# Convolution block 1 as four plain stretches ahead of the heads, with all of x prepared beside them

## The chip, the cores and the metric

One core of one Trainium2 chip runs the whole kernel. The metric is the device time of one execution in microseconds; the profile is one profiled execution on that core. Its engines are TensorE (PE), VectorE (DVE), ScalarE (ACT), GpSimd (POOL) and SyncE (SP), whose queue issues nearly all transfers of this kernel.

## The reference

One layer over 2048 tokens of width 1024, with 256 context tokens and a conditioning vector:

```python
shift, scale, gate = split(silu(c) @ w_ada + b_ada, 3)
h  = rmsnorm(x, norm_w) * (1 + scale) + shift
hc = rmsnorm(ctx, norm_w) * (1 + scale_c) + shift_c
p, pc = h @ w_in, hc @ w_in[:, :5 * 1024]        # w_in: 1024 x 9216
# 8 heads of 128: q, v, f_f, f_b and a gate; a gated linear recurrence in both directions,
# its start state from the context
y_hg = norm(o) * silu(gate)
# 8 convolution blocks of 128 channels, columns h, b, c, gate:
y_cv = b * conv3(c * h, along rows of 64) * silu(gate)
x = x + gate * (concat(y_hg, y_cv) @ w_out)
return rmsnorm(x, final_norm_w)
```

## The kernel before

The tokens stand in four groups of 512 (x0 to x3). Each group's normed h is transposed, so that a product has 128 columns of w_in as weights and tokens as the moving side. Every number is kept as two f16 parts (hi and lo), and a product is three f16 matmuls: hi·hi, hi·lo, lo·hi.

Two columns of 128 against the two halves of a group form a 2x2 block product, done in one of two ways. *Seven* (function `seven`) is a Strassen form: seven products instead of eight, on sums of weights (A11, A12, A22, S1 to S4) and sums of tokens: B11, T1, T2, B21, T3, B22, T4. A unit of seven is 7 x 4 x 3 = 84 matmuls, 256 wide in a head stretch; in a "pair" stretch of the convolution two groups run together, 512 wide. *Plain* needs no sums, only the hi and lo of h itself.

The token operands of the sevens lie in DRAM (`Hd`, rows of them by `ROWS`). A stretch loads its seven in "hops" of 512 KB ahead of use (`prefetch`; nine places). They are made from h32 by DVE subtractions and by casts on ACT or POOL: `turn` for a group that comes fresh from its transposes, `late_turn` for one whose h32 was put into DRAM (`Xd`) and is loaded again. Each has eight k-steps for D of 1024, or four pairs k, k+4: four (late) turns per group.

The program is a list of stretches ("windows"), and each has PE units, the chain of the scan and extra steps (norms, turns, weights' preparation), which are dealt out among the matmuls at fixed shares of the stretch. What is written in that order stands in that order on each engine, and every engine runs its row in order. Stretches 0 to 3 are head 0 on groups 0 to 3, then heads 1 to 7, convolution block 0 (four stretches), and blocks 1 to 7 as two "pair" stretches each. Head 0's stretches 0 and 1 are plain (256 wide) out of tiles in SBUF, since the sevens' operands do not exist yet; beside them x1 to x3 and the context are normed and turned, and scans of head 0 run. Groups 0 and 1 get their T operands by late turns in stretches 3 to 6. `gate_sums` (the residual's gate, eight `wg` loads of 512 KB, four with PE sums `gate_r` in stretch 2's first part and four in its second) run beside. Results leave PSUM by ACT (p, u) and by DVE (f, z, K and others); PE can use a bank again after that.

Names: `xT_x` transposes; `h_x` normed groups; `hop2T`: hop of stretch 2, T row; `sa`, `sb`, `sc`: banks of sevens; `u`: bank of plain or context products; `ws_p`: weights from DRAM; `whia_p`, `wloa_p`, `e_p` and so on: their parts; `ss_p`: the small matmul for a pair's scale; `ha_x`, `hb_x`, `hc_x`: what late turns load; `hpT_x`: what they store.

Of the kernel before, what the change touches and what calls it, by code (L numbers as in the profile page):

```python
# [31 lines left out]
VQ_AT = 3  # L32
SMALL = {"cc": 16, "bada": 16, "nw": 8, "lg": 32, "onw": 1, "cw": 24}
# [27 lines left out]
def hybrid_layer(ctx: ExitStack, tc, x, cx, w_ada, b_ada, w_in, w_out, fnorm_w, small_d, masks, ident_d, sel_d, out):  # L61
# [19 lines left out]
    ROWS = (("B11", "T3"), ("T1", "T2"), ("B21", "B22"), ("T4",))  # L81
# [3 lines left out]
    Xd = [dp.tile([P, KT, GW], F32, name=f"Xd{g}", tag=f"Xd{g}") for g in range(2)]  # L85
# [155 lines left out]
    def norm_group(ntile, src, row0, m, nm, first_ops=None, space=q_tile):  # L241
# [4 lines left out]
        before = None if opening else "x0" if m else f"x{row0 // GW - 1}"  # L246
# [58 lines left out]
        def store(op, k, src, eng):  # L305
            if m:
                i = ("B1", "B2", "D").index(op)
                hi, lo = hc[:, i, 0, k], hc[:, i, 1, k]
            else:
                hi, lo = [first_ops[k // 2][:, k % 2, i] for i in range(2)]  # L310
            cast(eng, hi, src)
            low.append(V.tensor_tensor(lo, src, hi, ALU.subtract))

        def store2(ops, k, row, eng):

            n2 = len(ops)
            pair = hp.tile([P, n2, 2, HW], F16, tag="pair", name=f"hp{ops[0]}_{nm}{k}", bufs=4)
            hi, lo = pair[:, :, 0], pair[:, :, 1]
            row = row.rearrange("p (a b) -> p a b", a=n2)
            cast(eng, hi, row)  # L320
            low.append(V.tensor_tensor(lo, row, hi, ALU.subtract))
            g = row0 // GW
            if n2 == 2:
                SY.dma_start(Hr[g][ops][:, :, k], pair)
            else:
                SY.dma_start(Hd[g][ops[0]][:, k], pair[:, 0])

        made = {}

        def rows_ahead(k):  # L330
            made[k] = rows(k), rows(k + HK)

        def turn(k):
            a, b = made.pop(k) if k in made else (rows(k), rows(k + HK))
# [7 lines left out]
            if first_ops is not None:  # L342
                for kk, h32 in ((k, a), (k + HK, b)):
                    SY.dma_start(Xd[row0 // GW][:, kk], h32)
                    store(None, kk, h32, S if kk < HK else G)
                return
            combine(k, a, b, True)

        def late_turn(k):
            a, b = ring(f"ha_{nm}{k}"), ring(f"hb_{nm}{k}")  # L350
            for kk, h32 in ((k, a), (k + HK, b)):
                SY.dma_start(h32, Xd[row0 // GW][:, kk])
            combine(k, a, b, False)
            late_done[row0 // GW] += 1
            prefetch()

        def combine(k, a, b, whole):
            b11, b12, b21, b22 = a[:, :HW], a[:, HW:], b[:, :HW], b[:, HW:]
            t = ring(f"ht_{nm}{k}")
            t1, t2 = t[:, :HW], t[:, HW:]  # L360
            V.tensor_tensor(t1, b12, b11, ALU.subtract)
# [8 lines left out]
            V.tensor_tensor(b21, b21, t2, ALU.subtract)  # L370
            store2(("T4",), k, b21, G)
# [5 lines left out]
                [lambda k=k: raw(k, pa_t if k < KT - 2 else px_t) for k in range(KT)],  # L377
                [paced(0.0, lambda k=k: rows_ahead(k)) for k in range(HK)])
# [16 lines left out]
    def load_pair(col0, col1, nm, own=False, a21_at=None):  # L395
# [47 lines left out]
        def sum_b():  # L443
# [4 lines left out]
                  part("S2", lambda: a11), sum_b, part("S3", lambda: a21), part("S4", lambda: a12)]  # L448
        block = col0 // P - 5 * HEADS
# [389 lines left out]
    class Conv:  # L839


        def __init__(s, b, groups):
            s.b, s.groups, s.nm = b, groups, f"{b}_{groups[0]}"
            s.n = HW * len(groups)
            s.cv = [None, None]
# [4 lines left out]
        def conv(s, i, u):  # L850
# [8 lines left out]
                                   ALU.mult, ALU.add)  # L859

# [366 lines left out]
    for wi, (kind, a, i) in enumerate(stretch):  # L1227
        units, chain, extra = [], [], []
        if kind == "head":
# [28 lines left out]
        else:
# [41 lines left out]
        if kind == "pair":  # L1300
            n = (a - 1) * 2 + i
# [91 lines left out]
    late_done = {0: 0, 1: 0}  # L1393
    plain = [[hp.tile([P, 2, 2, GW], F16, tag="hop", name=f"hop{g}_{i}") for i in range(KT // 2)] for g in range(2)]
    x1_norm = norm_group(NCH, x, GW, 0, "x1", plain[1], stage_tile)
    a21_ = hop_tile("a21")
    ga21 = scp.tile([P, 2, HK, P], F16, tag="Tsec", name="ga21", bufs=5)
    extra_a21 = [[[a21_[:, :, hl, i * P:(i + 1) * P] for hl in range(2)] for i in range(2)], [[ga21[:, 0], ga21[:, 1]]]]
    taken[0] = HOPS

    first = norm_group(NCH, x, 0, 0, "x0", plain[0])
# [10 lines left out]
    ctx_norm = norm_group(2, cx, 0, 1, "c")  # L1412
    for _, st in ctx_norm[0] + x1_norm[0]:
# [34 lines left out]
    def cost(u):  # L1448
        return {"head": 7 * HK, "conv": 7 * HK, "ctx": KT, "plain": 2 * KT, "pair": 14 * HK}[u[1]]

    ui = 0

    def run(wi, units, steps):
        nonlocal ui
        total = sum(cost(u) for u in units) - (0 if units[-1][1] in ("ctx", "plain") else cost(units[-1]) // 7)
# [18 lines left out]
        for un, (wk, kind, i, fn) in enumerate(units):  # L1474
# [22 lines left out]
            elif kind == "plain":  # L1497
                ps = bank(turn_bank[0], f"u{ui}")
# [186 lines left out]
```

## Time and profile before

| | us |
|---|---|
| median of three runs | 2150.36 (2148.98 to 2151.59) |
| span of the profiled execution | 2150.1 |
| PE busy | 2073.2 (96%) |
| DVE busy | 1645.8 (77%) |
| ACT busy | 1192.2 (55%) |
| POOL busy | 191.8 (9%) |
| mean granted TensorE clock | 0.994 |

Rows of groups and of the timeline give the time (or the count and busy time), the engine, the line of the kernel, the operation, what it writes and reads, and in brackets how long the engine was idle ahead of it and what ended that. A matmul's own duration overlaps that of the next; the distance of two starts is its price. Line numbers are those of the kernel before; the changed kernel's are a few to sixteen higher.

### The profile page before, as it was taken

The numbers are of one execution on the slowest core, as the hardware profiler recorded it, in microseconds if no ns is written. First come the engines' busy times: TensorE is split into PE (matmuls) and PEld (weight loads), VectorE is DVE, ScalarE is ACT, GpSimd is POOL, SyncE is SP. The second block draws the span as 40 slices with busy tenths as digits, with TensorE's granted clock in tenths as the row PEclk, the third lists the DMA queues.
The fourth block names the chain that finished last, engine by engine and source line by source line (L and its number), as shares of the span: only waits on it lengthen the run. The fifth ranks groups of instructions, "written<-read, shape, count | busy, mean of one in ns | idle before, by whom it ended". The sixth has DMA issues, their size and how long they took to land.

```text
span 2150.1 us, 53050 instructions
## 1 busy us (share of the span) xinstructions
PE 2073.2 (96%) x22111; PEld 1466.0 (68%) x22111; DVE 1645.8 (77%) x3413; ACT 1192.2 (55%) x2406; POOL 191.8 (9%) x272
## 2 busy tenths in 40 slices
PE   5988999999999999999999999999999999999998
PEld 2877878888888888888888887444444444444443
DVE  6787988878778787788687887678778656687775
ACT  7965666757567666576676654354445423333332
POOL 0121111111111110111110100000000000000000
PEclk9999999999999999999999999999999999999999
DMA  9567533442344233424543458933442105642421
GB/s 356 191 207 265 178 126 134 137 158 72 114 129 146 97 114 109 153 81 142 194 131 127 130 165 260 285 108 110 134 149 93 54 23 196 206 143 92 137 79 59
DMA packets 185798, 311.02 MB, mean 145 GB/s; under 512 B 13010, under 2 KB 114770, under 8 KB 183764
## 3 DMA queue, kind: packets, MB, share of 16 engines
q1 hardware_dynamic: 183396, 303.68, 42.9%
q8 instruction: 173, 2.83, 0.5%
q10 hardware_dynamic: 2160, 3.93, 0.5%
q14 instruction: 69, 0.57, 0.1%
HBM read 240.19 MB, written 67.37 MB: 143 GB/s over the span
## 4 chain that ended last, share of the span: by engine, by line
PE 65%; DVE 18%; ACT 7%; DMA 4%; issue 3%; POOL 1%; SPq 0%; POOLq 0%; ACTq 0%; DVEq 0%
PE sa L930 8%; PE sa L932 8%; PE sa L931 8%; PE sb L930 4%; PE sb L932 4%; PE sb L931 4%; PE sa_o L930 2%; PE sa_o L931 2%; PE sa_o L932 2%; DVE Q L492 2%; PE sc L930 2%; PE sc L931 2%; PE sc L932 2%; DVE K L485 2%; PE T L681 2%
## 5 line engine op out<-in xcount | busy, mean ns | idle before, releaser
L931 PEld LDWEIGHTS <-e_p 128*128 128x128 f16 x1332 | 130.4, 98 | 59.8 <-issue 10.3
L930 PEld LDWEIGHTS <-e_p 128*128 128x128 f16 x1332 | 130.4, 98 | 54.0 <-issue 1.1
L601 ACT ACTIVATE km<-K 128x512 f32<-128x512 f32 x192 | 129.6, 675 | 67.2 <-DVE K L485 61.1
L932 PEld LDWEIGHTS <-e_p 128*128 128x128 f16 x1332 | 130.3, 98 | 51.4
L485 DVE TENSOR_TENSOR K<-K,tot 128x512 f32<-128x512 f32 x192 | 132.2, 689 | 42.9 <-ACT km L601 25.3
L492 DVE TENSOR_TENSOR Q<-Q,tot 128x512 f32<-128x512 f32 x192 | 132.5, 690 | 34.9 <-POOL qm L608 19.5
L608 POOL COPY qm<-Q 128x512 f32<-128x512 f32 x96 | 80.8, 842 | 794.4 <-DVE Q L492 778.7
L931 PEld LDWEIGHTS <-whib_p 128*128 128x128 f16 x888 | 86.9, 98 | 42.1 <-issue 8.8
L930 PEld LDWEIGHTS <-whib_p 128*128 128x128 f16 x888 | 86.8, 98 | 36.7 <-issue 0.8
L930 PEld LDWEIGHTS <-whia_p 128*128 128x128 f16 x888 | 87.0, 98 | 35.7 <-DMA hop3B<-Hd3B 2.3
L932 PEld LDWEIGHTS <-wloa_p 128*128 128x128 f16 x888 | 87.0, 98 | 34.2
L931 PEld LDWEIGHTS <-whia_p 128*128 128x128 f16 x888 | 87.0, 98 | 33.9 <-issue 1.5
L932 PEld LDWEIGHTS <-wlob_p 128*128 128x128 f16 x888 | 86.8, 98 | 34.0
L157 ACT ACTIVATE e_p<-ws_p,sc_p 128x512 f16<-128x512 f32 x108 | 77.5, 718 | 54.9 <-DVE ws_p L444 42.0
L665 POOL COPY A<-Ac 32x128 f32<-32x128 f32 x128 | 77.2, 603 | 128.3 <-ACT A L661 110.6
L853 ACT ACTIVATE cv<-c,small 128x512 f32<-128x512 f32 (+1 forms) x36 | 24.2, 673 | 106.8 <-DVE c L871 61.1
L937 ACT ACTIVATE u<-sa,sx_w 128x256 f32<-128x256 f32 (+1 forms) x111 | 58.1, 524 | 43.5 <-PE sa L932 34.7
L937 ACT ACTIVATE p<-sa,sx_w 128x256 f32<-128x256 f32 (+1 forms) x111 | 57.4, 517 | 39.9 <-PE sa L932 39.8
L158 DVE SCALAR_TENSOR_TENSOR e_p<-ws_p,sc_p,e_p 128x512 f16<-128x512 f32 x108 | 79.4, 750 | 0.0
L409 ACT ACTIVATE junk<-ws_p 128x1024 f16<-128x1024 f32 x72 | 75.7, 1052 | 6.5 <-DMA ws_p<-in_w_in 6.3
L1596 POOL TENSOR_TENSOR x_o<-x_o,fw 128x512 f32<-128x512 f32 x1 | 1.3, 1262 | 868.0 <-ACT junk L1587 868.0
L937 ACT ACTIVATE p<-sb,sx_w 128x256 f32<-128x256 f32 (+1 forms) x111 | 57.8, 521 | 30.8 <-PE sb L932 28.0
(858 smaller groups left out, 7036.3 us busy)
## 6 DMA issues: line engine op xcount, KB each, us to landing
ws_p<-in_w_in SPq DMA_DIRECT2D x72, 512.0 KB, 4.3
y_o<-yT SPq DMA_DIRECT2D x32, 512.0 KB, 4.3
xt_x<-in_x SPq DMA_DIRECT2D x16, 512.0 KB, 6.2
wa<-in_w_ada SPq DMA_DIRECT2D x16, 512.0 KB, 10.2
Gd<-zs SPq DMA_DIRECT2D x32, 256.0 KB, 2.7
sg<-Gd SPq DMA_DIRECT2D x32, 256.0 KB, 4.4
wos<-in_w_out SPq DMA_DIRECT2D x32, 256.0 KB, 5.0
yT<-y SPq DMA_DIRECT2D x32, 256.0 KB, 2.9
```

What stands on the lines that cost most here:

```text
L157: S.activation(hi, src, AF.Copy, scale=st[:, 0:1])
L158: V.scalar_tensor_tensor(lo, src, st[:, 0:1], hi, ALU.mult, ALU.subtract)
L409: S.activation(junk.rearrange("p (k n) -> p k n", k=KT), stage[i], AF.Abs, accum_out=r)
L485: V.tensor_tensor(m, m, sub(cur, nb + 1, [[2, np_], [-(nb + 1), 2], [0, B]]), ALU.mult)
L492: V.tensor_tensor(m, m, sub(cur, 1, [[2, np_], [nb - 1, 2], [0, B]]), ALU.mult)
L601: S.activation(sub(s.km, 0, [[2 * B, n // (2 * B)], [B, 2], [1, B]]), mix(s.K, n, B, n // (2 * B)), AF.Copy)
L608: G.tensor_copy(sub(qm, 0, [[2 * B, n // (2 * B)], [B, 2], [1, B]]), mix(s.qf, n, B, n // (2 * B)))
L665: G.tensor_copy(A3[js, :, js], s.Ac[js])
L930: PE.matmul(ps, hi[:, k], rh, start=start and k == 0, stop=False, skip_group_check=not start)
L931: PE.matmul(ps, hi[:, k], right(name, 1, k), start=False, stop=False, skip_group_check=not start)
L932: PE.matmul(ps, lo[:, k], rh, start=False, stop=k == nk - 1, skip_group_check=not start)
L937: last_keep.append(S.activation(r, ps, AF.Copy, scale=sx))
```

## The change

Block 1 of the convolution leaves the "pair" stretches and becomes four new stretches ("open") ahead of head 0, one for each group. Each has two units of two products, plain, 512 wide (8 x 3 = 24 matmuls a product), evacuated by `open_first` and `open_second`. Their weights are the plain hi and lo, in tiles borrowed from the scan's pools (`homes`). Beside the four stretches run x1, x2, x3 and the context's norms and turns: now every group is cast plainly, kept in `Xd` and stored as B11, B21, B22 (`store_plain`). All T operands of all four groups come from 16 late turns of a new form: four loads, DVE subtractions, one POOL subtraction, and all casts on POOL. They stand in stretches 1 to 6. Heads 0 to 7 follow as stretches 4 to 35, all with sevens; head 0's first stretch starts without scan work. `gate_sums` moves to the last part of stretch 3, and its last sums come in stretch 4's first unit.

```diff
-    ROWS = (("B11", "T3"), ("T1", "T2"), ("B21", "B22"), ("T4",))
+    ROWS = (("T4", "T2"), ("T1", "T3"), ("B11",), ("B21", "B22"))
...
         def late_turn(k):
+            g = row0 // GW
             a, b = ring(f"ha_{nm}{k}"), ring(f"hb_{nm}{k}")
-            for kk, h32 in ((k, a), (k + HK, b)):
-                SY.dma_start(h32, Xd[row0 // GW][:, kk])
-            combine(k, a, b, False)
+            c_ = u_tile(f"hc_{nm}{k}")
+            SY.dma_start(b, Xd[g][:, k])
+            for r in range(2):
+                SY.dma_start(a[:, r * HW:(r + 1) * HW], Xd[g][:, k + r * HK, HW:])
+            SY.dma_start(c_, Xd[g][:, k + HK, :HW])
+            V.tensor_tensor(b, a, b, ALU.subtract)
+            V.tensor_tensor(a[:, HW:], a[:, HW:], b[:, :HW], ALU.subtract)
+            store2(("T1", "T3"), k, b)
+            G.tensor_tensor(a[:, :HW], c_, a[:, HW:], ALU.subtract)
+            store2(("T4", "T2"), k, a)
...
-    stretch = [("head", hd, i) for hd in range(HEADS) for i in range(NG)]
+    stretch = [("open", OPEN_B, g) for g in range(NG)]
+    stretch += [("head", hd, i) for hd in range(HEADS) for i in range(NG)]
...
-    stretch += [("pair", b, tp) for b in range(1, 8) for tp in range(2)]
+    stretch += [("pair", b, tp) for b in range(OPEN_B + 1, 8) for tp in range(2)]
...
+        elif kind == "open":
+            units.append((wkey(c0 + 2 * 1024, c0), kind, i, cvx.open_first))
+            units.append((wkey(c0 + 1024, c0 + 3 * 1024), kind, i, cvx.open_second))
...
-            elif n == 10:
+            elif n == 9:
                 extra += gate_steps()
-            elif n == 13:
+            elif n == 11:
                 extra += [paced(w_, put_next) for w_ in (0.35, 0.35, 0.15, 0.15)]
...
-            elif kind == "plain":
...
+            elif kind == "open":
+                for r, put in enumerate(fn(w)):
+                    ps = bank(open_bank[0], f"u{ui}{r}")
...
+                        PE.matmul(ps, op[0][:, kk], rh[0], start=k == 0, stop=False)
+                        PE.matmul(ps, op[0][:, kk], rh[1], start=False, stop=False)
+                        PE.matmul(ps, op[1][:, kk], rh[0], start=False, stop=k == KT - 1)
...
             if wi == 0:
+                early += x1_norm[1] + x1_norm[2][:1] + x2_norm[0] + x1_norm[2][1:] + x2_norm[1][:-1]
             elif wi == 1:
+                early += x2_norm[1][-1:] + x3_norm[0] + x2_norm[2] + x3_norm[1][:-1] + late_[0][:2]
+            elif wi == 2:
+                stage_free.append(True)
+                next_w(0, 2)
+                early += x3_norm[1][-1:] + ctx_norm[0] + x3_norm[2] + ctx_norm[1][:-1] + late_[0][2:]
             else:
+                next_w(0, 2)
                 sums = gate_sums()
+                early += (ctx_norm[1][-1:] + ctx_norm[2] + sums[:1] + late_[1][:2] + sums[1:2] + late_[1][2:3]
+                          + sums[2:])
...
+        elif wi == NG:
+            extra = late_[1][3:] + late_[2][:2] + [paced(0.1, lambda: next_w(1, 1))] + late_[2][2:3] + extra
+        elif wi == NG + 1:
+            extra = late_[2][3:] + late_[3][:2] + extra
+        elif wi == NG + 2:
+            extra = late_[3][2:] + extra
```

In the rows that follow, a tile's name has its own number behind it. The four late turns of group 1 are called x10 to x13 (turns 0 to 3 in the prediction). DVE before, at the start of stretch 3: two evacuations of f (head 0, group 3), and between them late turn x10 among scan work.

```order
L941 SCALAR_TENSOR_TENSOR f_0_3_2573<-sa_16_2575,sx_w0_482,p5_16_2652 128x256
L361 TENSOR_TENSOR ht_x10_2622<-ha_x10_2618 128x256
L492 TENSOR_TENSOR Q_0_2_2411<-Q_0_2_2411,tot_0_2_2639 128x64x2x4
L362 TENSOR_TENSOR ht_x10_2622<-hb_x10_2619,ht_x10_2622 128x256
L364 TENSOR_TENSOR ha_x10_2618<-hb_x10_2619,ha_x10_2618 128x256
L370 TENSOR_TENSOR hb_x10_2619<-hb_x10_2619,ht_x10_2622 128x256
L639 COPY_PREDICATED Ac_0_2_2695<-mask_127,A2_0_2_2755 128x128
L321 TENSOR_TENSOR hpT1_x10_2625<-ht_x10_2622,hpT1_x10_2625 128x2x256
L321 TENSOR_TENSOR hpT3_x10_2630<-ha_x10_2618,hpT3_x10_2630 128x256
L321 TENSOR_TENSOR hpT4_x10_2635<-hb_x10_2619,hpT4_x10_2635 128x256
L639 COPY_PREDICATED Ac_0_2_2695<-mask_127,A2_0_2_2755 128x128
L941 SCALAR_TENSOR_TENSOR f_0_3_2573<-sb_16_2607,sx_w0_482,u2_16_2709 128x256
```

DVE after, from the second late turn of group 1 (x11) at the end of the opening to head 0's first evacuations of f; `sg_1_3` is the gate of the last opening product.

```order
L348 TENSOR_TENSOR hb_x11_1528<-ha_x11_1527,hb_x11_1528 128x512
L349 TENSOR_TENSOR ha_x11_1527<-ha_x11_1527,hb_x11_1528 128x256
L324 TENSOR_TENSOR hpT1_x11_1536<-hb_x11_1528,hpT1_x11_1536 128x2x256
L324 TENSOR_TENSOR hpT4_x11_1541<-ha_x11_1527,hpT4_x11_1541 128x2x256
L869 SCALAR_TENSOR_TENSOR sg_1_3_1608<-u71_1519,sx_w1_583,sg_1_3_1608 128x512
L348 TENSOR_TENSOR hb_x12_1572<-ha_x12_1571,hb_x12_1572 128x512
L870 TENSOR_TENSOR sg_1_3_1608<-sg_1_3_1608,cv0_1_3_1438 128x512
L349 TENSOR_TENSOR ha_x12_1571<-ha_x12_1571,hb_x12_1572 128x256
L324 TENSOR_TENSOR hpT1_x12_1580<-hb_x12_1572,hpT1_x12_1580 128x2x256
L871 TENSOR_REDUCE ymax_130<-sg_1_3_1608 128x2
L324 TENSOR_TENSOR hpT4_x12_1585<-ha_x12_1571,hpT4_x12_1585 128x2x256
L957 SCALAR_TENSOR_TENSOR f_0_0_1621<-sc_8_1689,sx_w8_1618,p1_8_1658 128x256
```

Two late turns (x11 and x12) now stand ahead of head 0's first evacuation f, with the opening's last gate between them, and a third (x13, the rows behind these) ahead of the second evacuation.

SP before, at the same place of stretch 3: two hop loads, the scan's Gd stores, and the loads of two late turns.

```order
L1389 DMA hop3B22_2564<-Hd3B21_101 128x2048
L1389 DMA hop3T4_2566<-Hd3T4_102 128x2048
L795 DMA Gd0_105<-zs0_2_2569 128x512
L795 DMA Gd1_106<-zs1_2_2601 128x512
L352 DMA ha_x10_2618<-Xd1_104 128x512
L352 DMA hb_x10_2619<-Xd1_104 128x512
L1389 DMA hop5B11_3323<-Hd2B11_95 128x2048
L352 DMA ha_x11_2823<-Xd1_104 128x512
L352 DMA hb_x11_2824<-Xd1_104 128x512
L1389 DMA hop5T1_3325<-Hd2T1_96 128x2048
```

SP after: the stores of late turn x11 (`Hd1T1`, `Hd1T4`), the last gate loads `wg6` and `wg7`, the loads and stores of x12, and the hops of head 0's first stretch (`hop4`) among them.

```order
L325 DMA Hd1T1_92<-hpT1_x11_1536 256x1x512
L325 DMA Hd1T4_91<-hpT4_x11_1541 256x1x512
L1096 DMA wg6_1566<-in_w_ada 128x1024
L1096 DMA wg7_1568<-in_w_ada 128x1024
L344 DMA hb_x12_1572<-Xd1_104 128x512
L346 DMA ha_x12_1571<-Xd1_104 128x256 x2
L347 DMA hc_x12_1573<-Xd1_104 128x256
L1399 DMA hop4B22_1614<-Hd0B21_90 128x2048
L1109 DMA Gr_139<-gate_rows_1603 128x512
L1399 DMA hop4T4_1616<-Hd0T4_87 128x2048
L325 DMA Hd1T1_92<-hpT1_x12_1580 256x1x512
L873 DMA yT3_118<-sg_1_3_1608 128x512
```

The loads of a late turn now stand behind the stores of the one before, with gate loads between them.

PE before, in stretch 2: gate sums behind transposes of x3, among products of T2.

```order
L274 MATMUL xT_x36_2221<-ident_121,xt_x30_1371 128x128
L274 MATMUL xT_x36_2221<-ident_121,xt_x31_1373 128x128
L274 MATMUL xT_x36_2221<-ident_121,xt_x32_1586 128x128
L274 MATMUL xT_x36_2221<-ident_121,xt_x33_1588 128x128
L1087 MATMUL gate_r_2228<-wg0_1871,sc32_124 32x512 x2
L1087 MATMUL gate_r_2228<-wg1_1873,sc32_124 32x512 x2
L1087 MATMUL gate_r_2228<-wg2_1875,sc32_124 32x512 x2
L1087 MATMUL gate_r_2228<-wg3_1877,sc32_124 32x512 x2
L930 LDWEIGHTS e_p8_274
```

PE after, in head 0's first stretch: the last four pairs of gate sums stand between the second product (`sc`, B21) and the third (`sa`, B11).

```order
L946 MATMUL sc_8_1689<-hop4B21_1277,whia_p24_1088 128x256
L947 LDWEIGHTS whia_p24_1088
L947 MATMUL sc_8_1689<-hop4B21_1277,whia_p24_1088 128x256
L948 LDWEIGHTS wloa_p24_1089
L948 MATMUL sc_8_1689<-hop4B21_1277,wloa_p24_1089 128x256
L1103 MATMUL gate_r_1553<-wg4_1562,sc32_126 32x512 x2
L1103 MATMUL gate_r_1553<-wg5_1564,sc32_126 32x512 x2
L1103 MATMUL gate_r_1553<-wg6_1566,sc32_126 32x512 x2
L1103 MATMUL gate_r_1553<-wg7_1568,sc32_126 32x512 x2
L946 LDWEIGHTS whia_p24_1088
L946 MATMUL sa_8_1623<-hop4B11_1253,whia_p24_1088 128x256
```

The sums have moved by two stretches, from the middle of a stretch to the boundary at which late turns are done.

More of the change, by code (lines that the diff above doesn't have):

```diff
@@ L309, in store, with store2 @@
             else:
-                hi, lo = [first_ops[k // 2][:, k % 2, i] for i in range(2)]
+                hi, lo = [plain[row0 // GW][k // 2][:, k % 2, i] for i in range(2)]
             cast(eng, hi, src)
[L312 to L317, printed above, removed]
-            hi, lo = pair[:, :, 0], pair[:, :, 1]
[L319 to L331, printed above, removed]
+            if op is None and not opening and k in (1, 4, 6):
+                G.tensor_tensor(lo, src, hi, ALU.subtract)
+            else:
+                low.append(V.tensor_tensor(lo, src, hi, ALU.subtract))
+        def store2(ops, k, row):
+            pair = hp.tile([P, 2, 2, HW], F16, tag="pair", name=f"hp{ops[0]}_{nm}{k}", bufs=4)
+            hi, lo = pair[:, :, 0], pair[:, :, 1]
+            row = row.rearrange("p (a b) -> p a b", a=2)
+            cast(G, hi, row)
+            V.tensor_tensor(lo, row, hi, ALU.subtract)
+            SY.dma_start(Hr[row0 // GW][ops][:, :, k], pair)
         def turn(k):
-            a, b = made.pop(k) if k in made else (rows(k), rows(k + HK))
+            a, b = rows(k), rows(k + HK)
             if m:
@@ L448, in load_pair @@
                   part("S2", lambda: a11), sum_b, part("S3", lambda: a21), part("S4", lambda: a12)]
+        if homes is not None:
+            w.rest = [begin] + [lambda i=i: split(w.st, stage[i], *t["h"][2 * i:2 * i + 2]) for i in range(2)]
         block = col0 // P - 5 * HEADS
@@ L1330, in load_ahead @@
     def load_ahead():
-        if todo[0] and not ahead and not loaded[-2].rest and ready[0] >= NG - 1:
+        if todo[0] and not ahead and not loaded[-2].rest and stage_free:
             ahead.append(load(0))
@@ L1391, in prefetch, with plain_tiles @@
             taken[0] += 1
[L1393 to L1401, printed above, removed]
+    late_done = {g: 0 for g in range(NG)}
+    plain = {}
+    def plain_tiles(g):
+        plain[g] = [hp.tile([P, 2, 2, GW], F16, tag="hop", name=f"hop{g}_{i}") for i in range(KT // 2)]
+    for g in range(2):
+        plain_tiles(g)
+    taken[0] = NG * KT // 2
+    first = norm_group(NCH, x, 0, 0, "x0")
     for _, st in first[0]:
@@ L1421, in hybrid_layer @@
     follow(lows["x0"][:3], lambda: affine(1, 7))
-    x_norm = [None, x1_norm] + [norm_group(NCH, x, g * GW, 0, f"x{g}", None, q_tile if g == 2 else stage_tile)
-                                for g in range(2, NG)]
+    x2_norm = norm_group(NCH, x, 2 * GW, 0, "x2", q_tile)
+    spare = [f_tile, k_tile, f_tile, k_tile]
+    x3_norm = norm_group(NCH, x, 3 * GW, 0, "x3", lambda nm: spare.pop(0)(nm))
+    ctx_norm = norm_group(2, cx, 0, 1, "c")
+    x_norm = [first, x1_norm, x2_norm, x3_norm]
     def store_plain(g):
@@ L1448, in cost @@
     def cost(u):
-        return {"head": 7 * HK, "conv": 7 * HK, "ctx": KT, "plain": 2 * KT, "pair": 14 * HK}[u[1]]
+        return {"head": 7 * HK, "conv": 7 * HK, "ctx": KT, "open": 4 * KT, "pair": 14 * HK}[u[1]]
     ui = 0
+    open_bank = [0]
     def run(wi, units, steps):
         nonlocal ui
-        total = sum(cost(u) for u in units) - (0 if units[-1][1] in ("ctx", "plain") else cost(units[-1]) // 7)
+        total = sum(cost(u) for u in units) - (0 if units[-1][1] in ("ctx", "open") else cost(units[-1]) // 7)
         pace = [0, 0]
```

166 lines of the change are left out of this document (69 added, 97 removed).

## The prediction

> **What bounds the kernel now.** I read the page first, then busy time by stretches, then the waits and the timeline of the tensor engine (PE) up to 240 us, then DMA landings there. Page: busy time, and the 40 slices of 53.8 us.
>
> ```profile
> span 2150.1 us, 53050 instructions
> PE 2073.2 (96%) x22111; PEld 1466.0 (68%) x22111; DVE 1645.8 (77%) x3413; ACT 1192.2 (55%) x2406; POOL 191.8 (9%) x272
> PE   5988999999999999999999999999999999999998
> DMA  9567533442344233424543458933442105642421
> ```
>
> PE is the bound from the fifth slice on. Time can come from two places only: fewer or cheaper matmuls, or less PE idle time, which sits in the first four slices. Busy time by stretches (length, then busy PE, PEld, DVE, ACT, POOL; granted clock; DMA share; GB/s):
>
> ```profile
> 41.30:230.20 188.90, 168.87 (x2106) 141.15 (x2106) 153.23 (x357) 134.25 (x241) 40.88 (x57) 0.97 0.65 221
> 268.61:408.69 140.08, 135.15 (x2096) 117.99 (x2094) 120.96 (x274) 94.36 (x211) 21.88 (x31) 1.00 0.43 145
> 408.69:552.63 143.94, 141.95 (x2178) 126.03 (x2176) 114.76 (x255) 90.96 (x204) 19.87 (x28) 1.00 0.37 121
> 1900.00:2000.00 100.00, 100.00 (x466) 45.33 (x465) 76.34 (x143) 34.31 (x49) 0.00 (x0) 1.00 0.33 105
> ```
>
> The first row runs from head 0's first product to head 1's first: 188.90 - 168.87 = 20.0 us idle. The second is a period of four head stretches that still holds late turns: 4.9 idle. The third is one without them: 2.0. The last has 512-wide products at 100.00 / 466 = 0.2146 us each. What PE waited for in the first of these stretches (total, times, longest):
>
> ```profile
> PE sb L930 <- DVE f L941: 3.0, 2, 1.7
> PE u L1505 <- ACT hop L303: 2.1, 1, 2.1
> PE sa L930 <- DMA hop3B<-Hd3B: 2.1, 1, 2.1
> PE xT_x L274 <- DVE xt_x L267: 2.0, 2, 1.5
> PE u L1506 <- DVE hop L312: 1.9, 3, 1.0
> ```
>
> There is no single culprit: evacuations by the vector engine (DVE), a load of hops, transposes that wait for their norm. The rest is scan work.
>
> **Matmuls.** The 256-wide product issues each 0.109 us: of these two rows the second is the twelfth of a run, (143.24 - 142.04) / 11.
>
> ```profile
> 142.04 0.27 PE L930 MATMUL sb<-hop2T,whib_p 128*128 128x256 f16 x1
> 143.24 0.27 PE L932 MATMUL sb<-hop2T,wlob_p 128*128 128x256 f16 x1
> ```
>
> Removed: ten plain units of head 0 (48 each), 480 x 0.109 = 52.3 us; the two "pair" stretches of block 1, 2 x 2 x 84 = 336 x 0.2146 = 72.1. Added: four opening stretches of two units of four products of 24 in all, 4 x 4 x 24 = 384 x 0.2146 = 82.4; head 0's five units with sevens, 5 x 84 = 420 x 0.109 = 45.8. Sum: 128.2 - 124.4 = **+3.8 us**. Transposes, gate sums and scans are the same in number. Block 1 goes from a place where PE is 100% busy, so that these 72.1 us are fully won and the 82.4 fully paid.
>
> **Idle that goes.** All of the 20.0 us before head 1 is struck, **-20.0**; what the new stretches idle is added term by term. Head 1 no longer has late turns beside it: 4.9 - 2.0, **-2.9**. The opening's two pairs are split with no sums for sevens, which shortens the weights' preparation ahead of the first product a little; it then still waits for the conditioning and the first cast (2.1 in the waits), so **-0.5**, between 0 and -1. The moved wo steps, gate steps and last loads lie one or two pair stretches from where they were, beside DVE at 76% and ACT at 34% busy, with PE at 100.00 in 100 (the last window row): nothing; uncovered, they would cost what they take, a few us.
>
> **Opening stretches (0 to 3).** First products: three units run interleaved at 512 wide, so PE needs each new cast half as often; of 1.9 us behind L1506, 1.0. In stretch 1 the transposes of x2 wait for its norm, which stands on DVE among evacuations: 2.0 measured in two places, I take 1.7. In stretch 2 the next pair's weight load is issued on SP behind T stores: nearest row the 2.1 behind hop3B, 2.0. In stretch 3 ctx's transposes wait likewise: 1.5. Together **+6.2**; both ends: 2 (only first products and one wait) and 12 (each of the four twice).
>
> **Late turns at head 0's first stretch.** This decides. Head 0's first group now needs all of its T operands from DRAM, and group 1's must follow one stretch later; so turns run at the boundary, on DVE, GpSimd (POOL) and SP, with gate sums among them. The precedent before is the boundary at 187 us:
>
> ```profile
> 187.16 5.09 SPq L795 DMA_DIRECT2D Gd<-zs  x2
> 192.36 0.61 SPq L352 DMA_DIRECT2D ha_x<-Xd  x1
> 199.69 0.43 DVE L361 TENSOR_TENSOR ht_x<-ha_x 128x256 f32<-128x256 f32 x1 [2.60 <-DMA ha_x<-Xd]
> 202.49 0.40 POOL L301 TENSOR_SCALAR hpT_x<-hb_x 128x256 f16<-128x256 f32 x1 [1.03 <-DVE hb_x L370]
> 204.22 0.47 DVE L941 SCALAR_TENSOR_TENSOR f<-sb,sx_w,u 128x256 f32<-128x256 f32 x1
> 204.75 0.27 PE L930 MATMUL sb<-hop3T,whib_p 128*128 128x256 f16 x1 [1.25 <-DVE f L941]
> ```
>
> SP sits 5.09 us at a store that waits; the late load behind it issues at 192.36 and reaches DVE at 199.69, 7.3 later; the turn keeps DVE until the evacuation f, queued behind it, at 204.22, and that one holds PE until 204.75. In the new order this is chained. Durations for a turn and its neighbours:
>
> ```profile
> L435 DVE TENSOR_TENSOR ws_p<-ws_p,ws_p 128x512 f32<-128x512 f32 x5 | 3.4, 689 | 0.1
> L321 DVE TENSOR_TENSOR hpT_x<-ht_x,hpT_x 128x512 f16<-128x512 f32 x16 | 11.7, 729 | 2.3 <-ACT hpT_x L303 2.2
> L301 POOL TENSOR_SCALAR hop<-h_x 128x512 f16<-128x512 f32 x8 | 6.2, 782 | 10.3 <-ACT h_x L296 9.7 <-ACT h_x L292 0.5
> L1596 POOL TENSOR_TENSOR x_o<-x_o,fw 128x512 f32<-128x512 f32 x1 | 1.3, 1262 | 868.0 <-ACT junk L1587 868.0
> 173.28 0.60 ACT L1092 ACTIVATE gate_rows<-gate_r 128x512 f32<-128x512 f32 x1 [0.93 <-PE gate_r L1087]
> wg<-in_w_ada SPq DMA_DIRECT2D x4, 512.0 KB, 5.1
> hb_x<-Xd SPq DMA_DIRECT2D x4, 256.0 KB, 4.3
> ```
>
> A turn is subtract 0.69, POOL cast 0.78, POOL subtract of 256 (half of 1.26) 0.63, POOL cast 0.78, DVE low part 0.73, with four hand-overs of 0.1: 4.0 us, because DVE and POOL alternate. Let t be the nominal start of head 0's first stretch. The evacuation of the third product of stretch 3 comes one product (24 x 0.2146 = 5.2) before t; with ctx's last two steps DVE is free for the turns at about t - 4. Turns 0 and 1 of group 1: to t + 4. SP then stores turn 1's rows, and behind that store issues the last two gate loads (wg6, wg7): landed t + 4 + 0.6 + 5.1 = t + 10. PE needs them after 24 products (2.6) and six earlier gate sums (0.7): at t + 3.5, so **a first stall of 6.5**. Then gate_rows 0.6 and the sigmoid of the opening's last product on ACT, its DVE multiply, and only then turn 2: t + 13 to t + 17. Its store releases turn 3's loads on SP: t + 22; turn 3 ends at t + 26, and behind it stands the evacuation f<-sa without which A22·T4 can't use its bank. PE reaches that product at t + 10 + 48 x 0.109 = t + 15: **a second stall of 11**. Together 17.5; with the faster end of each row (loads 4.3, turns 3.4) 12; if the loads of group 1 themselves land 4 us late behind the hop loads, 21. The least that holds even with idle DVE: wg6 may be issued only when the sums before it have read its buffer (t + 2), so 4. I take **+16**. Behind a stall PE is slow for a while:
>
> ```profile
> 136.96 2.12 PE L274 MATMUL xT_x<-ident,xt_x 128*128 128x128 f32 x8 [1.55 <-DVE xt_x L267]
> 139.09 0.42 PE L931 MATMUL sa<-hop2B,whia_p 128*128 128x256 f16 x1
> 141.65 0.33 PE L930 MATMUL sa<-hop2B,whia_p 128*128 128x256 f16 x1
> ```
>
> The products show 0.42 instead of 0.27 until 141.65, thirteen at half pace: 13 x 0.109 = 1.4 us lost for a short idle; I add **+1.5**, at most 3 for two stalls. The Trainium skill ("TensorE: Matmul & The Clock Gate", Part 1) says that one idle window of about 3.4 us drops the clock to half and about 3.4 us of work restores it. By that, as an estimate, two stalls would cost 2 x 1.7 = 3.4 and the sum would be 9.7; the trace's half pace after an idle of 1.55 was shorter, 2.8 us.
>
> Head 0's other three stretches carry the turns of groups 2 and 3, as head 1 did: 4.9 x 3/4 = **+3.7**.
>
> **Sum.** 3.8 - 20.0 - 2.9 - 0.5 + 6.2 + 16 + 1.5 + 3.7 = **+7.8**. The profiled span is 2150.1, the median of the runs 2150.36: 2158.
>
> **A rule against the change.** All casts of late turns and one subtraction move to POOL. Beside casts on POOL, DVE's subtractions were slow, and they recovered behind them:
>
> ```profile
> 41.53 4.13 DVE L312 TENSOR_TENSOR hop<-h_x,hop 128x512 f16<-128x512 f32 x4
> 45.66 1.28 DVE L312 TENSOR_TENSOR hop<-h_x,hop 128x512 f16<-128x512 f32 x2
> 41.30 1.80 POOL L301 TENSOR_SCALAR hop<-h_x 128x512 f16<-128x512 f32 x2
> ```
>
> 1.03 against 0.64 each. The Trainium skill ("SBUF — State Buffer", Who interferes with whom) has it that a DVE instruction with two SBUF inputs and a GpSimd one that reads SBUF lock each other out of a shared port pair. By it each overlap lengthens a turn by up to 0.4, some 1.5 us over four turns; the sum leaves that out, because within a turn the two alternate.
>
> **Rivals.** (a) *The turns keep up*, and the time falls. POOL is 9% busy and DVE loses the scans in these stretches; if late loads land in 4.3 and turns overlap, the stall shrinks to the 4 of the gate loads, with 0.5 of clock: 7.8 - 12 - 1 = -5, with opening waits at their low end (-4) -9: 2141 to 2147. It decides if turn 1 has ended by t. Against it: the order puts four turns ahead of the evacuation on an in-order DVE. (b) *It cancels*: stall 9 or so, one hop of the chain hidden: 7.8 - 7 = +1, 2151. (c) *DMA becomes the bound*. Up to the T4 load of head 0's first stretch some 38 MB must move in about 110 us (the bytes of the transfers in SP's order), 346 GB/s, where the first row of the stretches had 221. What mixed traffic reached at full share:
>
> ```profile
> 165.00:170.00 5.00, 5.00 (x102) 4.32 (x100) 4.46 (x11) 1.07 (x2) 2.49 (x5) 1.00 0.98 343
> 190.00:200.00 10.00, 10.00 (x207) 8.69 (x205) 4.41 (x8) 6.62 (x14) 1.17 (x1) 1.00 1.04 373
> ```
>
> At 343 every stretch of the opening runs at the limit and the loads of x3, ctx and weights fall behind by about 10 us more: 2168 and above. For it: no slack; against it: most loads have a stretch of lead.
>
> **Chances.** Forecast 0.5 (2154.7 to 2167), (a) 0.24, (b) 0.16, (c) 0.1. A measurement of this kernel tells 0.2% from no change, 2146.1 to 2154.7. The range reaches into (a) and to the edge of (c): 2142 to 2168. Faster 0.24, same 0.16, slower 0.60.
>
> **What the profile after would show.** Right: PE idle a few us ahead of gate_r with wg loads as releaser; a longer wait of sa on DVE f within head 0's first stretch, some 12 to 20 us together; SP waiting at the T stores; a low clock behind; the second conv stretch gone from the end and 3.8 us more PE busy. Wrong: turns of group 1 finished before the last opening product; waits that sit elsewhere, as at ss_p or at the transposes in stretches 1 and 2; or a DMA share near 1 from 60 us on, which is (c).

## The result, and the profile after

The changed kernel takes 2188.53 us (median of four runs, 2185.9 to 2191.23) against 2150.02; ratio 1.0184, 95% interval 1.0169 to 1.0198: slower by 39 us, where 8 were forecast and 18 was the end of the range. The profiled execution of it has a span of 2184.6, 34.5 above that of before.

Page of the changed kernel, span, busy time, slices (54.6 us each) and DMA share:

```profile
span 2184.6 us, 53035 instructions
PE 2088.9 (96%) x22099; PEld 1469.7 (67%) x22099; DVE 1637.5 (75%) x3348; ACT 1175.6 (54%) x2373; POOL 238.1 (11%) x319
PE   6987899999999999999999999999999999999998
DMA  9988644333533344234443452885433424633321
```

PE is busy 15.7 us longer and idle 18.8 us longer. The holes are in the third to fifth slices. To place the difference I use a step that both kernels run once per head, in that head's first stretch: the evacuation of the context's value (`vT_c`) on ACT. First the three rows of before (heads 1, 2 and 7), then those of the changed kernel:

```profile
268.61 0.47 ACT L550 ACTIVATE vT_c<-u,sx_w 128x256 f32<-128x256 f32 x1
408.69 0.47 ACT L550 ACTIVATE vT_c<-u,sx_w 128x256 f32<-128x256 f32 x1
1135.94 0.47 ACT L550 ACTIVATE vT_c<-u,sx_w 128x256 f32<-128x256 f32 x1
```

```profile
378.56 0.48 ACT L537 ACTIVATE vT_c<-u,sx_w 128x256 f32<-128x256 f32 x1
515.58 0.47 ACT L537 ACTIVATE vT_c<-u,sx_w 128x256 f32<-128x256 f32 x1
1240.66 0.47 ACT L537 ACTIVATE vT_c<-u,sx_w 128x256 f32<-128x256 f32 x1
```

Up to this row of head 1 the changed kernel is 109.95 us later, to head 2 106.89, to head 7 104.72, at the end 34.5. So from head 1 to head 2 it wins 3.1, to head 7 2.2 more, and 70.2 behind that, where 72.1 us of products left. The loss lies ahead of that row of head 1: the opening and head 0 brought 128.2 - 52.3 = 75.9 us of products, and took 110. Busy time from the first product to head 1's row, before:

```profile
41.29:268.61 227.32, 205.59 (x2661) 173.52 (x2661) 189.38 (x437) 160.43 (x293) 46.88 (x66) 0.98 0.65 219
```

And after, with its two worst windows of 20 us:

```profile
40.31:378.56 338.25, 294.24 (x2986) 210.05 (x2986) 242.24 (x481) 177.38 (x318) 96.35 (x116) 0.93 0.69 221
160.00:180.00 20.00, 8.91 (x29) 2.55 (x30) 7.51 (x11) 1.72 (x4) 5.12 (x7) 0.55 0.71 229
180.00:200.00 20.00, 14.89 (x97) 11.30 (x97) 9.31 (x18) 7.30 (x13) 4.95 (x7) 0.76 0.79 250
```

Idle time of PE went from 227.32 - 205.59 = 21.7 to 44.0: **+22.3**. Busy time rose by 88.7, and 75.9 of that are products: **+12.8** are products at a lower clock (0.55 and 0.76 in the two worst windows, 0.93 over all, 0.98 before) and gate sums. With the first product 1.0 earlier this is the 110.

PE at head 0's start, timeline of the changed kernel (the first row is the stretch's first product):

```profile
152.73 0.27 PE L946 MATMUL sb<-hop4T,whib_p 128*128 128x256 f16 x1
165.72 1.92 PE L1103 MATMUL gate_r<-wg,sc 128*32 128x512 f32 x4 [4.40 <-DMA wg<-in_w_ada]
171.44 3.21 PE L1103 MATMUL gate_r<-wg,sc 128*32 128x512 f32 x8 [3.79 <-DMA wg<-in_w_ada]
176.70 0.37 PE L946 MATMUL sa<-hop4B,whia_p 128*128 128x256 f16 x1 [2.06 <-DVE sg L869]
190.64 0.37 PE L946 MATMUL sa<-hop4T,whib_p 128*128 128x256 f16 x1 [5.03 <-DVE f L957]
```

With 1.48 and 0.19 ahead of earlier gate sums and 0.56 before another product these are 17.5 us, the total that the prediction worked out, but in other parts. The gate loads hold PE four times, for 9.9 in all, and what stands behind them for 7.6; the prediction had one wait of 6.5 and one of 11. The links of the chain stand where it put them, first on SP, then on DVE:

```profile
163.94 1.72 SPq L325 DMA_DIRECT2D Hd1T<-hpT_x  x2
165.76 1.04 SPq L1096 DMA_DIRECT2D wg<-in_w_ada  x2
181.81 0.61 SPq L344 DMA_DIRECT2D hb_x<-Xd  x1
186.12 0.69 DVE L348 TENSOR_TENSOR hb_x<-ha_x,hb_x 128x512 f32<-128x512 f32 x1 [4.50 <-DMA ha_x<-Xd]
190.10 0.48 DVE L957 SCALAR_TENSOR_TENSOR f<-sa,sx_w,p 128x256 f32<-128x256 f32 x1
```

The last two gate loads issue at once behind turn 1's stores; turn 3's loads behind turn 2's; and f behind turn 3, at 190.10, for a product that starts at 190.64. That product stands 37.9 us behind the stretch's first, where the prediction had 26 (its t + 15 and a stall of 11): the idle time is as summed, and the other 12 us are PE busy with gate sums in pieces and with products at half pace.

SP's row shows the price of the stores; what SP waited for longest between 40 and 230 us (total, times, longest):

```profile
SPq L325 <- DVE hpT_x L324: 30.5, 16, 5.4
```

What the prediction had not seen is how the same chain reaches on, into the next stretch (DVE, ACT, PE):

```profile
216.30 0.69 DVE L348 TENSOR_TENSOR hb_x<-ha_x,hb_x 128x512 f32<-128x512 f32 x1 [3.37 <-DMA ha_x<-Xd]
219.40 0.14 DVE L152 TENSOR_SCALAR sc_p<-ss_p 128x1 int32<-128x1 int32 x1
221.91 1.15 ACT L158 ACTIVATE whia_p<-ws_p,sc_p 128x1024 f16<-128x1024 f32 x1 [5.18 <-DVE sc_p L153]
223.58 0.45 ACT L953 ACTIVATE u<-sa,sx_w 128x256 f32<-128x256 f32 x1
224.09 0.37 PE L946 MATMUL sa<-hop5T,e_p 128*128 128x256 f16 x1 [4.59 <-ACT u L953]
```

DVE waits for a late load; the scale of the next weights stands behind that turn on DVE; the weight's cast waits for the scale at the head of ACT's row; and the evacuation u, which needs none of these, stands behind the cast. PE waits 4.59 us for a load that it does not use. From stretch 5's first `hop5B` product to head 1's context value:

```profile
213.17:378.56 165.39, 151.25 (x2214) 131.25 (x2212) 127.56 (x261) 87.36 (x168) 36.88 (x46) 0.97 0.51 159
```

PE idles 165.39 - 151.25 = 14.1 us there, in stretches 5 to 7.

### The profile page after: what moved, and what is told of

It reads as the page before. It is cut to its first block, busy times and chain, and to the rows that moved or that the text cites. A ratio compares the mean times of both kernels' runs of the same rounds, so it can differ in the third digit from the quotient of the medians.

```text
span 2184.6 us, 53035 instructions
## 1 busy us (share of the span) xinstructions
PE 2088.9 (96%) x22099; PEld 1469.7 (67%) x22099; DVE 1637.5 (75%) x3348; ACT 1175.6 (54%) x2373; POOL 238.1 (11%) x319
## 4 chain that ended last, share of the span: by engine, by line
PE 56%; DVE 12%; ACT 6%; DMA 2%; issue 2%; POOL 1%; POOLq 0%; ACTq 0%; DVEq 0%
PE sa L946 7%; PE sa L948 7%; PE sa L947 7%; PE sb L946 3%; PE sb L948 3%; PE sb L947 3%; PE sa_o L946 2%; PE sa_o L948 2%; PE sa_o L947 2%; PE sc L946 2%; PE sc L948 2%; PE sc L947 2%; PE A L618 1%; DVE Q L479 1%; PE T L668 1%
## 5 line engine op out<-in xcount | busy, mean ns | idle before, releaser
L947 PEld LDWEIGHTS <-e_p 128*128 128x128 f16 x1344 | 132.3, 98 | 60.6 <-issue 15.7
L946 PEld LDWEIGHTS <-e_p 128*128 128x128 f16 x1344 | 132.2, 98 | 48.8 <-issue 0.2
L948 PEld LDWEIGHTS <-e_p 128*128 128x128 f16 x1344 | 132.3, 98 | 46.9
L479 DVE TENSOR_TENSOR Q<-Q,tot 128x512 f32<-128x512 f32 x192 | 132.9, 692 | 39.0 <-POOL qm L595 22.3
L159 DVE SCALAR_TENSOR_TENSOR e_p<-ws_p,sc_p,e_p 128x512 f16<-128x512 f32 x102 | 74.9, 745 | 0.0
L158 ACT ACTIVATE hiS_o<-y_o,sc_y 128x1024 f16<-128x1024 f32 x32 | 36.8, 1148 | 69.8 <-PE sa_o L947 32.1
```

The costliest lines, as they stand in the source:

```text
L158: S.activation(hi, src, AF.Copy, scale=st[:, 0:1])
L159: V.scalar_tensor_tensor(lo, src, st[:, 0:1], hi, ALU.mult, ALU.subtract)
L479: V.tensor_tensor(m, m, sub(cur, 1, [[2, np_], [nb - 1, 2], [0, B]]), ALU.mult)
L946: PE.matmul(ps, hi[:, k], rh, start=start and k == 0, stop=False, skip_group_check=not start)
L947: PE.matmul(ps, hi[:, k], right(name, 1, k), start=False, stop=False, skip_group_check=not start)
L948: PE.matmul(ps, lo[:, k], rh, start=False, stop=k == nk - 1, skip_group_check=not start)
```

## The experiments

All change the changed kernel. Times are medians; beside them is the ratio to before, on the same chip, with its 95% interval in brackets. Rows whose intervals overlap can hardly be told apart. "To before" is the ratio less one, times 2150.

| run | us | ratio (interval) | to before |
|---|---|---|---|
| changed kernel | 2188.5 | 1.0184 (1.0169 to 1.0198) | +39.6 |
| no_late | 2133.8 | 0.9925 (0.9911 to 0.9940) | -16.1 |
| late_dma_only | 2153.5 | 1.0014 (1.0005 to 1.0024) | +3.0 |
| late_compute_only | 2156.6 | 1.0029 (1.0018 to 1.0040) | +6.2 |
| gate_sums_later | 2185.5 | 1.0167 (1.0150 to 1.0184) | +35.9 |
| loads_ahead | 2180.7 | 1.0143 (1.0128 to 1.0158) | +30.7 |
| sums_later_loads_ahead | 2178.1 | 1.0120 (1.0103 to 1.0136) | +25.8 |
| stores_off_sp | 2169.6 | 1.0076 (1.0059 to 1.0093) | +16.3 |
| direct_g2_g3 | 2187.8 | 1.0167 (1.0152 to 1.0182) | +35.9 |
| casts_on_act | 2183.8 | 1.0160 (1.0143 to 1.0177) | +34.4 |
| off_sp_casts_on_act | 2166.2 | 1.0081 (1.0066 to 1.0096) | +17.4 |
| off_sp_act_ctx_sums | 2169.1 | 1.0097 (1.0081 to 1.0114) | +20.9 |
| off_sp_act_ahead | 2167.5 | 1.0090 (1.0065 to 1.0114) | +19.4 |

**What the late turns cost, and in which half.** Three kernels take them apart. Without any:

```diff
-            a, b = ring(f"ha_{nm}{k}"), ring(f"hb_{nm}{k}")
...
-            store2(("T4", "T2"), k, a)
...
-            SY.dma_start(t, Hd[g_][o])
+            SY.dma_start(t, Hd[g_]["B11" if o[0] == "T" else o])
```

> Leaves out all sixteen late turns (their loads, DVE and POOL work and stores); every T hop is read from the B11 rows instead, so the output is not the reference's. Matmuls, hops, gate sums, norms are as in the changed kernel. Theory (late turns stand in the in-order rows of DVE and SP, and what is queued behind them comes late): the idle of PE behind ss_p (4.2), ctx's transposes (4.6), f (5.0, 2.6, 1.7), ACT u (4.6, 1.2), qm (2.7) goes, of the 12 at the gate sums some 4 stay because wg4 to wg7 still wait for PE to read wg0 to wg3; with some 8 of half clock 2188 falls by 30 to 38, to about 2150 to 2158. Rival (the gate sums alone hold PE at head 0's start, the rest is scan work): 2180. Rival (DMA is the bound up to 160 us): the loads of x, ctx, w stay, only 8 MB of 54 go: 2175 to 2183.

Only their transfers:

```diff
-            V.tensor_tensor(b, a, b, ALU.subtract)
...
-            store2(("T4", "T2"), k, a)
+            for ops in (("T1", "T3"), ("T4", "T2")):
+                SY.dma_start(Hr[g][ops][:, :, k], still[0])
```

> Late turns issue their four loads and two stores (of a constant tile, so the output is not the reference's), but have no DVE and POOL work, and no store waits for one. All bytes move as in the changed kernel. Theory (in-order rows): as without late turns, within 6 us, 2150 to 2162. Rival (DMA is the bound): no better than 2180, with PE waiting for DMA at the same places.

Only their arithmetic:

```diff
-            SY.dma_start(Hr[row0 // GW][ops][:, :, k], pair)
...
+            V.tensor_tensor(b, st, st, ALU.subtract)
+            V.tensor_tensor(a[:, HW:], st[:, HW:], b[:, :HW], ALU.subtract)
```

> The other half of late_dma_only: late turns do their DVE and POOL work on a constant tile, with no loads and no stores; T hops are read from the B11 rows, so the output is not the reference's. Theory (the 35 us between late_dma_only and the changed kernel are waits: DVE's row waits for late loads, SP's row for DVE, and evacuations and loads stand behind): 2134 to 2142, near the run without late turns. Rival (DVE and POOL occupancy, 16 turns of 4 us and the shared ports, is itself what holds PE): 2155 or more.

Without late turns the kernel is 16 us *faster* than before, further than I had expected: the rest of the change does win. The turns cost 39.6 + 16.1 = 55.7 us. Their transfers alone cost 19.1, their arithmetic alone 22.3, and the two together 14.3 more than the sum. So my theory, that only the coupling of rows costs, fell, although the time with transfers only lay in the range that I gave: both halves cost by themselves. Transfers first, busy time by stretches, without late turns and then with their DMA only (the last two columns are DMA share and GB/s):

```profile
140.00:180.00 40.00, 37.83 (x305) 26.95 (x304) 13.82 (x27) 16.18 (x32) 0.41 (x1) 1.00 0.56 205
180.00:220.00 40.00, 39.69 (x585) 35.23 (x583) 30.54 (x72) 23.56 (x46) 6.21 (x7) 1.00 0.39 126
```

```profile
140.00:180.00 40.00, 31.44 (x186) 16.62 (x185) 7.95 (x15) 10.42 (x20) 0.99 (x2) 0.91 0.96 328
180.00:220.00 40.00, 38.41 (x521) 32.96 (x522) 27.59 (x64) 24.66 (x50) 2.92 (x3) 1.00 1.01 346
```

With the turns' bytes the DMA engines are full up to 220 us at 328 and 346 GB/s, and PE is busy 31.4 of 40 in the first of the two instead of 37.8. But SP also has the turns' issues in its row: in the changed kernel two stores take it 1.72 us (163.94) and the four loads behind them 2.2, so that sixteen turns take some 63 us of SP, by estimate. Full DMA engines and a fuller SP were not tried apart; the 19 us are the price of both. Then the arithmetic, DVE with no loads at all, and what PE waits for longest there:

```profile
124.76 0.68 DVE L344 TENSOR_TENSOR hb_x<-still 128x512 f32<-128x512 f32 x1
125.81 1.10 DVE L344 TENSOR_TENSOR hb_x<-still 128x512 f32<-128x512 f32 x1
126.84 1.21 DVE L326 TENSOR_TENSOR hpT_x<-hb_x,hpT_x 128x512 f16<-128x512 f32 x1
```

```profile
PE xT_c L277 <- DVE sx_w L365: 6.2, 1, 6.2
PE xT_x L277 <- DVE xt_x L270: 5.2, 2, 4.4
```

The turns push the norms of x and the context back on DVE, and the same subtraction takes 0.68 or 1.10 as POOL is idle or busy.

**Links of the chain, one at a time.** Gate sums to head 0's last stretch:

```diff
-                early += (ctx_norm[1][-1:] + ctx_norm[2] + sums[:1] + late_[1][:2] + sums[1:2] + late_[1][2:3]
-                          + sums[2:])
+                early += ctx_norm[1][-1:] + ctx_norm[2] + late_[1][:3]
+        elif wi == NG + 3:
+            extra = gate_sums() + extra
```

> gate_sums moves from stretch 3 to stretch 7 (head 0's last), nothing else. Theory (chain of late turns, of which the gate loads are one link): the 9.9 us before gate_r and the 2.1 behind sg go, but turns 2 and 3 still stand before f, so that the wait there grows from 5 to about 10; with 2 of clock and 2 for sums that run in one piece: 2178 to 2183. Rival (the gate loads are the cause of the stall at head 0's start): the whole stall of 17.5 and 5 of clock go, 2165 or less.

Loads one turn ahead:

```diff
+            if (g, k) not in came:
+                late_load(k)
+            a, b, c_ = came.pop((g, k))
+            g2, k2 = (g, k + 1) if k + 1 < HK else (g + 1, 0)
+            if g2 < NG and (g, k) != (0, HK - 1):
+                loads_of[g2](k2)
```

> The four loads of a late turn are issued one turn ahead, before the turn ahead of it computes and stores, so that no load waits behind that turn's stores on SP. Theory (SP's order: loads behind stores cost one landing of 4 to 5 us per turn): the waits on f at 190 us (5.0), of DVE on ha_x (4.5, 2.1, 3.4) shrink, the gate loads stay as late: 2174 to 2182. Rival (DMA is the bound): the loads only land later, 2186 to 2190. Rival (DVE and POOL work itself): same, within 3 us.

Both:

> Both earlier edits together: gate_sums in stretch 7, and a late turn's loads issued one turn ahead. Theory (links of one chain): each alone only uncovered the next link, -3 and -8; both together free it, more than the sum, 2166 to 2174. Rival (DMA is the bound, whatever the order): the sum at best, 2177 or more.

Stores of late turns on another queue:

```diff
-            SY.dma_start(Hr[row0 // GW][ops][:, :, k], pair)
+            G.dma_start(Hr[row0 // GW][ops][:, :, k], pair)
```

> Late turns' stores are issued from POOL's queue instead of SP's, so that no load on SP waits behind a store that waits for DVE. Theory: the waits at ss_p (4.2), gate_r (9.9) and for ha_x behind stores shrink, 2170 to 2180. Rival (DMA bound, or DVE's row): 2185 or more. POOL would wait for DVE's low part 0.7 us in each store, and its own issue cost is not known, which could take back some.

What PE then waits for at head 0's start: gate sums later, loads ahead, both, and stores off SP (two rows):

```profile
PE sa L946 <- DVE f L957: 10.5, 3, 8.5
```

```profile
PE gate_r L1116 <- DMA wg<-in_w_ada: 13.0, 2, 10.8
```

```profile
PE sa L959 <- DVE sg L882: 11.0, 1, 11.0
```

```profile
PE sa L946 <- DVE f L957: 7.4, 4, 4.8
PE gate_r L1103 <- DMA wg<-in_w_ada: 0.5, 1, 0.5
```

As foretold, without gate loads the wait for f grew, to 8.5, and with earlier late loads the gate loads came later still (10.8). Each edit alone uncovered the next link: -3.7 us by the ratios, which the intervals hardly tell from nothing and which is less than expected, and -8.9; both together -13.8, hardly more than the sum. That is against my theory and above its range, and it fits the rival that had the DMA as bound (2177 or more). The one large gain is the stores: -23 us, with the gate loads' wait down from 9.9 to 0.5. SP's row, in which loads stand behind stores that wait for DVE (30.5 us in the row above), is the costliest of the links tried. The edit also takes the stores' issue time off SP, some 27 us by estimate (16 x 1.72); how much each of the two brought was not tried.

**Work moved between engines.** T rows of groups 2 and 3 in their turns:

```diff
+                if not whole:
+                    SY.dma_start(Xd[row0 // GW][:, kk], h32)
...
+                V.tensor_tensor(t1, a[:, HW:], a[:, :HW], ALU.subtract)
...
+                store2(("T4", "T2"), k, b)
```

> Groups 2 and 3 get their T rows in their turns, from h in SBUF: no store to Xd, no late loads (9.2 MB less), eight late turns less in stretches 4 to 6, the same DVE and POOL work in stretches 1 and 2 instead. Theory (waits for late loads and what stands behind them): the 12.8 us of idle in stretches 5 to 7 go with some clock, the turns of x2 and x3 cost a few us in stretches 1 and 2: 2168 to 2177. Rival (DVE occupancy): the opening takes what the heads give, 2183 to 2195.

Casts on ACT:

```diff
-            cast(G, hi, row)
+            S.activation(hi, row, AF.Copy)
```

> Late turns' hi casts go to ACT instead of POOL (POOL keeps its one subtraction). Rule of the shared port pair (a DVE subtraction beside a POOL cast took 1.08 to 1.21 us instead of 0.69): 16 turns x 2 overlaps x 0.4 us = 13 us less on DVE, of which the half in stretches 3 to 6 that holds PE: 2176 to 2184. Theory (chain of loads, stores and evacuations; the turn itself takes 4 us either way): 2184 to 2190, or slower, since casts then stand before evacuations on ACT's row.

> Stores of late turns on POOL's queue and casts on ACT. Where the two gains are independent, 2169.6 less the gain of casts_on_act. Theory (rows in order): POOL's row has then only a subtraction and the stores, DVE loses its slow overlaps: 2160 to 2168.

The first moves 9.4 MB less, has no late loads for two groups, and can't be told from the changed kernel (35.9 against 39.6). The waits moved from the heads to the opening, as the rival of DVE's occupancy had it: transposes of x waited up to 12.1 us for their norm. Behind that, from stretch 5's first product to head 1's context value:

```profile
232.50:379.92 147.42, 145.78 (x2217) 129.30 (x2216) 111.11 (x236) 89.09 (x172) 21.26 (x28) 1.00 0.36 119
```

Stretches 5 to 7 take 147.4 us instead of 165.4 for the same products. PE idles 1.6 instead of 14.1 and is busy 5.5 less, at a clock of 1.00 for 0.97. So the late turns of groups 2 and 3 cost 18 us there. Casts on ACT won 5 us by the ratios, at the border of what the two theories gave and with intervals that just overlap; ACT's own row took the place:

```profile
PE sa L946 <- ACT u L953: 8.4, 4, 6.9
PE sa L946 <- ACT p L953: 5.6, 3, 4.0
```

Added to the stores' edit they won nothing that can be told (1.0081 against 1.0076).

**Attempts at a better kernel.** Both start from stores off SP with casts on ACT. With the context's norm ahead of late turns of group 0 and gate sums later, and then with loads ahead instead:

```diff
-                early += x3_norm[1][-1:] + ctx_norm[0] + x3_norm[2] + ctx_norm[1][:-1] + late_[0][2:]
+                early += x3_norm[1][-1:] + ctx_norm[0] + x3_norm[2] + ctx_norm[1] + late_[0][2:]
```

> The same, and the context's norm ahead of the last two late turns of group 0 on DVE, and gate_sums in stretch 7. Theory: the 7.8 us at ctx's transposes go to 2, the gate loads' 4 MB leave the boundary: 2150 to 2160. Rival (DMA bound, 20 us as in late_dma_only): 2160 or more.

> Stores of late turns on POOL's queue, casts on ACT, and a late turn's loads issued one turn ahead: the three edits that each helped. Theory (waits for late loads on DVE's row are what is left): 2155 to 2162. Rival (DMA at its limit from 60 to 180 us, 20 us as in late_dma_only, so that earlier issue does not land earlier): 2163 to 2170.

Neither gained over stores_off_sp, as the rival with full DMA engines had it. No version that computes the layer beats the kernel before; the best is 16 us above it and 32 above the one without late turns.

## Why the prediction was wrong

- **Direction and place** held: slower, by waits at head 0's first stretch, in the order given (gate loads, sg, turn 2, turn 3, f). That stall measured 17.5, the step's own result; 16 was taken. That its total came out is in part luck: turn 1 was to end 4 us behind the stretch's first product and ended 12.4 behind it (165.1), as DVE had waited 5.54 for the load of turn 0, and the two parts measured 9.9 and 7.6 for 6.5 and 11.
- **Work**, +3.8: 75.9 us of products in and 72.1 out fit the rows; PE has 12 matmuls less (22099 for 22111), as 384 + 420 - 480 - 336 gives, and of the 72.1 us 70.2 show. **Head 1 without late turns**, -2.9: 3.1.
- **The first step that failed: "Head 0's other three stretches ... 4.9 x 3/4 = +3.7".** It took the price of late turns from a stretch of before and had them cost the same here. Those stretches idled 14.1: DVE waits for their loads (2.10 at 204.47, 3.37 at 216.30), and weights and evacuations of the next stretch stand behind them. That the turns of groups 2 and 3 are the cause is shown by the kernel that has none for them: 1.6. Why the same kind of work idled only 4.9 before was not tried.
- **The second: the clock, +1.5, and gate sums at nothing.** Together 12.8. The sums are the same in number, but run in pieces:

```profile
151.30 1.05 PE L1103 MATMUL gate_r<-wg,sc 128*32 128x512 f32 x4 [0.19 <-DMA wg<-in_w_ada]
L1103 PE MATMUL gate_r<-wg,sc 128*32 128x512 f32 x32 | 10.4, 776 | 9.9 <-DMA wg<-in_w_ada 9.9
160.18 1.92 PE L1087 MATMUL gate_r<-wg,sc 128*32 128x512 f32 x16
```

  Four by themselves take 1.05 at full clock, where sixteen in one piece took 1.92 before (last row): 10.4 in all against 3.8. The last twelve of the 10.4 ran at half clock, four in 1.92 and eight in 3.21, so that some 2.5 of the 6.6 more are the clock too. The other 6.2 of the 12.8 are put down to the clock because nothing else is left; in stretches 5 to 7 alone PE was 5.5 busier than without late turns of groups 2 and 3. How much of it stands on the path was not tried by itself.
- **The third: the opening, +6.2**, measured 1.7 (first products), 0.8 (x2), 4.2 (ss_p), 4.6 (context) = 11.3, near the upper end that it gave (12).
- Beyond their terms these three are 10.4, 11.3 and 5.1 us, and the stall 1.5: 28.3, where the span missed the forecast by 26.7.
- **Rivals.** That DMA becomes the bound had one chance in ten; it is true at most in part. Of the loss 19 us are there with the transfers alone, SP's issues among them, but its sign, a DMA share near 1 from 60 us on, is not clear: in windows of 20 us the changed kernel has 1.00 at 60, 0.83 at 120, 0.98 at 140 and 0.71 at 160. "The turns keep up" is false; without the turns' cost the time would have fallen, by 16 us. The rule on ports was left out of the sum with the reason that DVE and POOL alternate within a turn. They do not quite; these are DVE and POOL in the same turn:

```profile
162.72 1.20 DVE L324 TENSOR_TENSOR hpT_x<-hb_x,hpT_x 128x512 f16<-128x512 f32 x1 [0.51 <-POOL hpT_x L302]
162.65 0.72 POOL L351 TENSOR_TENSOR ha_x<-hc_x,ha_x 128x256 f32<-128x256 f32 x1
```

  DVE's first low part takes 1.20 for 0.69 beside POOL's subtraction. The turn as a whole still took the 4 us of the prediction (161.06 to 165.12), since it goes by POOL's row there; what is lost is DVE's time for other work. The range's upper end, 2168, lay below the sum of the steps' own upper ends (3.8 - 20.0 - 2.9 + 12 + 21 + 3 + 3.7 = 20.6, 2171), and even that sum misses the 10 us of stretches 5 to 7 and the gate sums.

## What to carry to other kernels

Where a change puts work with loads at its head and stores at its tail into in-order rows, price what stands behind it on every row, SP's above all, and follow the chain into the next stretches until it runs out; a precedent from another place in the order can price it too low. Count the bytes against the rate at which mixed traffic has run full, and the issues against the issuing queue's time; a demand equal to that rate deserves more than one chance in ten. To find where a loss comes from, run the new work as transfers alone, as arithmetic alone and not at all: three runs told more than six edits of the order.

## What was not expected of the hardware

Matmuls with 32 weight columns for different rows of a bank cost 0.12 us each in a run of sixteen (1.92) and 0.26 in fours between other products (1.05), both at a granted clock of 1.00. A DVE subtraction of 128x512 with two SBUF inputs took 0.68 us alone and 1.08 to 1.21 beside a POOL instruction that had started first; where DVE's had (178.52), it took 0.68, and POOL's subtraction behind it (178.69) 1.10 for 0.72. The Trainium skill ("SBUF — State Buffer", Who interferes with whom) states such an exclusive lock, and these rows agree. Taking the casts off POOL, though not the subtraction, was worth only 5 us of the 40.
